# A seventh z tile inside the sample attention, the eighth behind it, in a one-core hybrid decoder step

## The chip, the cores and the metric

The kernel runs on one core of a Trainium2 chip. The metric is the device time of one execution in microseconds (us), as the median of several runs.

## What is computed

One layer of a decoder: an RMS norm, one input projection of width 1024 to 5648, three groups (a gated linear recurrence, a dilated-window attention, a state-space block) each with a gate, and one output projection. A prompt of 2048 tokens starts from empty state; eight samples of four tokens continue from a cache of 1024 positions. The parts that matter here:

```python
u = h @ w_in
x_lru, g_lru, q, k, v, g_attn, z, xbc, dt_raw = jnp.split(u, offs, axis=-1)
...
parts = [band_attn_sample(qh, k_all, v_all, W, slopes, wd, dl) for (wd, dl) in DILATIONS]
...
yg = (ys.reshape(Bn, L, D_SSD) * jax.nn.silu(z.astype(f32)))
```

`z` is 1024 columns wide and needs nothing but the normed input and the weights; it is used only at the end, in the state-space block. The kernel therefore uses its projection as filler work for TensorE in stages that would otherwise leave it idle.

## The kernel before

All matrices of the projections are split into a high and a low part, and every product is three matmuls (lines 82, 83 and 84). z is cut into eight tiles of 128 columns, here called z0 to z7. A tile loads its 512 KB of weights (`wr`, line 143), scales them on GpSimd (line 146), rounds the high part on ScalarE (`wh`, line 147) and takes the low part on VectorE (`wl`, line 148). Its matmuls fall into five pieces, one for each stretch of tokens, in the order 512, 512, 256, 288 and 512 tokens; a piece is 24 matmuls. ScalarE applies SiLU to a piece (`zo`, line 636) and the sync engine SP stores it (`d_z`, line 637). `z_tile` is a generator that yields after each piece.

The generator `zs` holds the pieces of the tiles meant for filling. The stage that advances the samples' state takes 14 of them (two of every three of its 20 steps). The samples' attention then runs: `fills()` walks eight parts (two heads by four samples each) through 80 steps. A part loads its cached keys (`kc` and `kf`) and values (`vt` and `vf`) and a bias (`sbias`), transposes the keys (line 911), computes scores in four column tiles (`sc`, line 932: 512 recent keys, then 128 far ones, then 32 new ones), does a softmax, transposes the weights `p` (line 954), multiplies by the values (`so`, line 966) and turns the result (`om`, line 973); a store of `ys` to `d_y` ends it. A loop over these steps decides at which of them the next z piece is taken.

Behind the attention, `z_end` holds the z tiles that are left, then frees their pools and loads the exp table. While it is walked, the scores of the first prompt unit (lines 1103 and 1124) are put between its pieces. The prompt attention has sixteen units; `load(i)` asks for the keys `k`, queries `q` and, with every fourth unit, a 1184 KB bias of unit i; `scores(i)` is one of seven steps, `exps(i)` the softmax. The bias's buffer lies in the memory of the samples' attention, so its load waits for that to be given up; `k` and `q` take buffers of the input tiles, which come free as the last z tiles finish with them.

Nothing runs in the order written: a scheduler at build time places the instructions of each engine by priority (mostly the order of the code) and by its own idea of when each can run. On the chip each engine, and SP's queue of transfers, then goes through its own list strictly in that order.

Of the kernel before, what the change touches and what calls it, by code (L numbers as in the profile page):

```python
# [22 lines left out]
CHUNKS = [(0, 512), (512, 512), (1024, 512), (1536, 256), (1792, 288)]  # L23
# [9 lines left out]
def tile_hybrid_step(ctx: ExitStack, tc: tile.TileContext, A):  # L33
# [121 lines left out]
    def project_steps(c0, evac, scale=1.0, order=CHUNKS):  # L155

        wh, wl = load_w(c0, scale)
        for t0, n in order:
            h_, l_, cols = xt(t0, n)
            ps = psA.tile([128, 512], F32, tag="mm", name="mm")  # L160
            for k in range(8):
                mm3(ps[:, :n], wh[:, k], wl[:, k], h_[k // 2][:, k % 2, cols], l_[k // 2][:, k % 2, cols], k == 0, k == 7)
            now = later[:]
            later.clear()
            for f in now:
                f()
            evac(ps, t0, n)
            for g in behind:
                next(g, None)
            yield  # L170
# [462 lines left out]
    def z_tile(pl, m):  # L633
        def evac(ps, t0, n):
            zt = pl.tile([128, 512], F32, tag="zo", name="zo", bufs=2)
            z_last.append(act.activation(out=zt[:, :n], in_=ps[:, :n], func=AF.Silu))
            sp.dma_start(out=d_z[128 * m:128 * m + 128, t0:t0 + n], in_=zt[:, :n])
        yield from project_steps(C_Z + 128 * m, evac, order=[CHUNKS[i] for i in (2, 1, 3, 4, 0)])
# [131 lines left out]

    zo_es = ExitStack()
    zo = zo_es.enter_context(tc.tile_pool(name="zo", bufs=1))
    zs = (None for m in range(6) for _ in z_tile(zo, m))


    with tc.tile_pool(name="cks", bufs=1) as ck:
# [92 lines left out]
    with tc.tile_pool(name="sa", bufs=1) as sa:  # L869
# [112 lines left out]
        def fills():  # L982

            parts = [sample_part(pr, bg) for pr in range(4) for bg in range(2)]
            for i, part in enumerate(parts):
                for j in range(6):
                    next(part)
                    yield
                    if i and j < 4:
                        next(parts[i - 1])  # L990
                        yield
            for _ in parts[-1]:
                yield

        for i, _ in enumerate(fills()):
            if i % 5 == 0:
                next(zs, None)
        for _ in zs:
            pass
# [28 lines left out]
            yield  # L1028

    def z_end():  # L1030
        zs = [z_tile(zo, m) for m in (6, 7)]
        for _ in CHUNKS:
            for z in zs:
                next(z, None)
                yield
        for z in zs:
            for _ in z:
                pass
        zo_es.close()
        wp_es.close()  # L1040
        with tc.issue_after(z_last[-1].ins):
            exp_ln = act.preload_act_table_set("natural_log_exp_and_others")
        ctx.enter_context(tc.issue_after(exp_ln.ins))
# [299 lines left out]
    def load(i):  # L1343
        if i < 16:
            next(units[i])

    def scores(i):
        return i >= 16 or next(units[i]) == "S"
# [4 lines left out]
    load(0)  # L1353
    load(1)
    s0 = False
    for i, _ in enumerate(z_end()):
        if i >= 6:
            for _ in range(3):
                s0 = s0 or scores(0)
    while not s0:  # L1360
        s0 = scores(0)
    ptp = es.enter_context(tc.tile_pool(name="ptp", bufs=8))
    load(2)
    while not exps(0):
        pass
    while not scores(1):
        pass
    next(units[0])
    for i in range(16):
        load(i + 3)  # L1370
# [279 lines left out]
```

## Time and profile before

| | us |
|---|---|
| median of 3 runs | 1965.07 (1964.24 to 1966.66) |
| the profiled execution, its own time | 1966.87 |
| its span, first to last instruction | 1965.1 |
| PE (TensorE matmul) busy | 1906.4, 97% of the span |
| DVE (VectorE) busy | 1065.2, 54% |
| ACT (ScalarE) busy | 780.9, 40% |
| samples' attention | about 981 to 1137 of the span |
| z6 and z7 with the first prompt scores | about 1137 to 1185 |

The profile is of one execution. PE's busy time is modelled, so a busy PE is not PE at its peak; a place where it is idle, or where its granted clock falls, is what the table above does not show and the rows below do.

### The profile page before, as it was taken

The numbers are of one execution on the slowest core, as the hardware profiler recorded it, in microseconds if no ns is written. First come the engines' busy times: TensorE is split into PE (matmuls) and PEld (weight loads), VectorE is DVE, ScalarE is ACT, GpSimd is POOL, SyncE is SP. The second block draws the span as 40 slices with busy tenths as digits, with TensorE's granted clock in tenths as the row PEclk, the third lists the DMA queues.
The fourth block names the chain that finished last, engine by engine and source line by source line (L and its number), as shares of the span: only waits on it lengthen the run. The fifth ranks groups of instructions, "written<-read, shape, count | busy, mean of one in ns | idle before, by whom it ended". The sixth has DMA issues, their size and how long they took to land.

```text
span 1965.1 us, 35826 instructions
## 1 busy us (share of the span) xinstructions
PE 1906.4 (97%) x14178; PEld 1559.9 (79%) x14178; DVE 1065.2 (54%) x2338; ACT 780.9 (40%) x1530; POOL 271.9 (14%) x346
## 2 busy tenths in 40 slices
PE   7999999999999999999999899999998999999998
PEld 7998888888888888887866686777776878677876
DVE  7414444444423666664322215666777777667774
ACT  6412637272712222223133315666564333324332
POOL 0100111111110111111000100000012232322231
PEclk9999999999999999998999999999999999999999
DMA  7422121121223222225477651442375444434441
GB/s 234 127 83 67 46 65 54 55 76 55 76 83 95 72 78 67 72 68 148 139 199 201 185 185 52 145 137 77 116 216 156 140 128 128 124 110 131 124 140 65
DMA packets 278388, 222.03 MB, mean 113 GB/s; under 512 B 34738, under 2 KB 234402, under 8 KB 278220
## 3 DMA queue, kind: packets, MB, share of 16 engines
q1 hardware_dynamic: 278220, 219.73, 37.3%
q8 instruction: 112, 1.84, 0.4%
q14 instruction: 56, 0.46, 0.1%
HBM read 150.81 MB, written 68.86 MB: 112 GB/s over the span
## 4 chain that ended last, share of the span: by engine, by line
PE 85%; DMA 4%; ACT 4%; DVE 3%; issue 1%; SPq 1%; POOL 1%; DVEq 0%; ACTq 0%; POOLq 0%
PE mm L82 15%; PE mm L84 15%; PE mm L83 15%; PE ops L84 5%; PE ops L83 5%; PE ops L82 5%; PE pt L1179 3%; ACT sr L1151 2%; PE o L1215 2%; PE s L1124 2%; PE yd L1298 2%; PE yo L1303 1%; PE s L1103 1%; DMA x<-in_x_prompt_dram 1%; PE mmt L82 1%
## 5 line engine op out<-in xcount | busy, mean ns | idle before, releaser
L82 PE MATMUL mm<-xh,wh 128*128 128x512 f32 (+2 forms) x1600 | 563.3, 352 | 1.6 <-DVE h L846 0.9
L83 PE MATMUL mm<-xl,wh 128*128 128x512 f32 (+2 forms) x1600 | 561.7, 351 | 0.0
L84 PE MATMUL mm<-xh,wl 128*128 128x512 f32 (+2 forms) x1600 | 561.0, 351 | 0.0
L82 PEld LDWEIGHTS mm<-xh,wh 128*128 128x128 f32 x1600 | 301.7, 189 | 44.0 <-issue 4.3
L84 PEld LDWEIGHTS mm<-xh,wl 128*128 128x128 f32 x1600 | 300.9, 188 | 41.0 <-issue 2.9
L83 PEld LDWEIGHTS mm<-xl,wh 128*128 128x128 f32 x1600 | 301.4, 188 | 39.0 <-issue 1.7
L146 POOL TENSOR_TENSOR wr<-wr,gC 128x1024 f32<-128x1024 f32 x40 | 79.1, 1978 | 415.7 <-DMA wr<-in_w_in_dram 370.8
L443 DVE SCALAR_TENSOR_TENSOR o<-u,ssdc,o 128x512 f32<-128x512 f32 (+1 forms) x216 | 128.8, 617 | 5.1
L1151 ACT ACTIVATE sr<-sr,nm 128x384 f32<-128x384 f32 (+3 forms) x128 | 97.9, 771 | 23.3 <-DVE nm L1147 14.1
L650 ACT ACTIVATE o<-o 128x512 f32<-128x512 f32 (+2 forms) x60 | 33.1, 552 | 149.4 <-DVE o L443 77.3
L148 DVE SCALAR_TENSOR_TENSOR wl<-wr,wh 128x1024 fp32r<-128x1024 f32 x40 | 48.9, 1223 | 68.4 <-ACT wh L147 68.4
L1062 ACT COPY ptsb<-pt 128x512 f32<-128x512 f32 x96 | 52.5, 583 | 75.0 <-PE pt L1179 74.9
L728 DVE TENSOR_SCALAR sg<-sg,cum 128x128 f32<-128x128 f32 (+1 forms) x256 | 72.9, 344 | 16.5 <-ACT ecB L726 16.5
L82 PE MATMUL mmt<-wh,xh 128*128 128x256 f32 (+3 forms) x272 | 78.5, 291 | 1.6 <-ACT xh L254 0.8
L83 PE MATMUL mmt<-wl,xh 128*128 128x256 f32 (+3 forms) x272 | 77.8, 287 | 0.3
L1179 PE MATMUL pt<-ident,sr 128*128 128x128 f32 x576 | 75.2, 281 | 2.8 <-ACT sr L1151 1.8
L84 PE MATMUL mmt<-wh,xl 128*128 128x256 f32 (+3 forms) x272 | 77.9, 288 | 0.0
L1112 DVE CUSTOM_DVE_ANT_1 sr<-s,bias 128x256 f32<-128x256 f32 x128 | 46.5, 419 | 56.9 <-PE s L1124 29.7
L441 DVE TENSOR_SCALAR o<-u,ssdc 128x512 f32<-128x512 f32 (+1 forms) x72 | 40.5, 575 | 65.8 <-ACT u L423 57.6
L1179 PEld LDWEIGHTS pt<-ident,sr 128*128 128x128 f32 x576 | 63.6, 143 | 15.1 <-issue 8.8
L423 ACT COPY u<-mm 128x512 f32<-128x512 f32 (+1 forms) x80 | 39.6, 495 | 88.6 <-PE mm L84 79.6
L726 ACT ACTIVATE ecB<-sg 64x512 f32<-64x512 f32 x60 | 37.8, 630 | 91.7 <-DMA sg<-d_cum 77.1
(526 smaller groups left out, 3585.0 us busy)
## 6 DMA issues: line engine op xcount, KB each, us to landing
wr<-in_w_in_dram SPq DMA_DIRECT2D x40, 512.0 KB
sg<-d_cum SPq DMA_DIRECT2D x30, 512.0 KB
d_xbc<-o SPq DMA_DIRECT2D x36, 256.0 KB
x<-in_x_prompt_dram SPq DMA_DIRECT2D x32, 256.0 KB
kc<-in_cache_attn_k_dram SPq DMA_DIRECT2D x32, 256.0 KB
vt<-in_cache_attn_v_dram SPq DMA_DIRECT2D x32, 256.0 KB
xres<-in_x_prompt_dram SPq DMA_DIRECT2D x32, 256.0 KB
out_dram<-ot SPq DMA_DIRECT2D x32, 256.0 KB
```

The lines of the kernel that those rows point to most:

```text
L82: pe.matmul(out, lhsT=wh, rhs=xh, start=start, stop=False)
L83: pe.matmul(out, lhsT=wh, rhs=xl, start=False, stop=False)
L84: pe.matmul(out, lhsT=wl, rhs=xh, start=False, stop=stop)
L146: pool.tensor_tensor(out=wr, in0=wr, in1=gC[:, :, None].to_broadcast([128, 8, 128]), op=OP.mult)
L148: dve.scalar_tensor_tensor(out=wl, in0=wr, scalar=scale, in1=wh.bitcast(F32), op0=OP.mult, op1=OP.subtract)
L441: dve.tensor_scalar(out=o, in0=v(0), scalar1=w[:, 0:1], scalar2=b, op0=OP.mult, op1=OP.add)
L443: dve.scalar_tensor_tensor(out=o, in0=v(t), scalar=w[:, t:t + 1], in1=o, op0=OP.mult, op1=OP.add)
L728: dve.tensor_scalar(out=sg[:n, h], in0=sg[:n, h], scalar1=cum[:n, c, 8 * g + h:8 * g + h + 1], scalar2=0.0, op0=OP.subtract, op1=OP.min)
L1062: act.copy(out=out, in_=in_)
L1112: dve.tensor_tensor_reduce(out=sr[e][r][:, nk:].rearrange("p (w c) -> p w c", w=2), in0=pw[e][:, j].rearrange("p (w c) -> p w c", w=2), in ...
L1151: act.activation(out=sr[e][r], in_=sr[e][r], func=AF.Exp, bias=nm[:, e, r:r + 1], accum_out=ll[:, e, r:r + 1])
L1179: pe.transpose(tp[:, r], sr[e][r][:, 128 * g:128 * g + 128], ident)
```

## The change

Seven tiles instead of six go into `zs`, the loop over the 80 attention steps takes 21 pieces instead of 16, evenly spread, and `z_end` has one tile in place of two that took turns. The scores of the first prompt unit may start after the second piece of z7 instead of the seventh of ten, and once they are through, those of the second unit may be taken between the pieces too.

```diff
-    zs = (None for m in range(6) for _ in z_tile(zo, m))
+    zs = (None for m in range(7) for _ in z_tile(zo, m))
...
         for i, _ in enumerate(fills()):
-            if i % 5 == 0:
+            if i * 21 % 80 < 21:
                 next(zs, None)
...
     def z_end():
-        zs = [z_tile(zo, m) for m in (6, 7)]
-        for _ in CHUNKS:
-            for z in zs:
-                next(z, None)
-                yield
-        for z in zs:
-            for _ in z:
-                pass
+        yield from z_tile(zo, 7)
...
     s0 = False
+    s1 = False
     for i, _ in enumerate(z_end()):
-        if i >= 6:
+        if i >= 1:
             for _ in range(3):
-                s0 = s0 or scores(0)
+                if not s0:
+                    s0 = scores(0)
+                elif i >= 4:
+                    s1 = s1 or scores(1)
...
-    while not scores(1):
-        pass
+    while not s1:
+        s1 = scores(1)
```

No instruction of the computation is added or removed. What moves is the order on the engines, and three places of it carry the prediction.

SP's list around the weights of z5, before. `wr` is that load; `d_z` is the store of z4's last piece; `kf`, `vt` and `vf` belong to the sixth part, `d_y` is the fifth part's result, and the rows behind `wr` are the seventh part's.

```order
L637 DMA d_z<-zo 128x512
L893 DMA kf<-in_cache_attn_k_dram 32x4x128 x4
L887 DMA vt<-in_cache_attn_v_dram 128x4x128 x4
L979 DMA d_y<-ys 128x16
L893 DMA vf<-in_cache_attn_v_dram 32x4x128 x4
L143 DMA wr<-in_w_in_dram 128x8x128
L899 DMA sbias<-in_c_sbias_dram 128x672
L887 DMA kc<-in_cache_attn_k_dram 128x4x128 x4
```

The same place of the changed kernel; the first `d_z` is z4's fourth piece, the second its last, and the other rows are the fifth part's.

```order
L899 DMA sbias<-in_c_sbias_dram 128x672
L887 DMA kc<-in_cache_attn_k_dram 128x4x128 x4
L637 DMA d_z<-zo 128x288
L143 DMA wr<-in_w_in_dram 128x8x128
L893 DMA kf<-in_cache_attn_k_dram 32x4x128 x4
L637 DMA d_z<-zo 128x512
L887 DMA vt<-in_cache_attn_v_dram 128x4x128 x4
```

The load stood behind the store of z4's last piece and thirteen further transfers; it now stands one piece ahead of that store.

PE's list where z4 ends, before: the last matmul of z4, then one whole part of the attention, then z5.

```order
L84 MATMUL mm<-xh_103,wl 128x512
L911 MATMUL tp<-ident,kc 128x128 x8
L954 MATMUL tp<-ident,p 128x128 x5
L954 MATMUL tp<-ident,p 32x128
L911 MATMUL tp<-ident,kc 128x128 x4
L966 MATMUL so<-vt,pt 32x128 x16
L966 MATMUL so<-vf,pt 32x128 x4
L966 MATMUL so<-vsn,pt 32x128 x4
L911 MATMUL tp<-ident,kc 128x128 x4
L973 MATMUL tp<-ident,om 128x128
L932 MATMUL sc<-ktT,qz 32x512
L911 MATMUL tp<-ident,kf 128x128 x4
```

The end of z4 in the changed kernel, and z5 from `xh_108` on.

```order
L84 MATMUL mm<-xh_103,wl 128x512
L911 MATMUL tp<-ident,kc 128x128 x4
L966 MATMUL so<-vt,pt 32x128 x16
L966 MATMUL so<-vf,pt 32x128 x4
L966 MATMUL so<-vsn,pt 32x128 x4
L911 MATMUL tp<-ident,kc 128x128 x4
L82 MATMUL mm<-xh_108,wh 128x512
L83 MATMUL mm<-xl_124,wh 128x512
L932 MATMUL sc<-ktT,qz 32x512
```

z5 follows z4 after half a part instead of a whole one with no filler in it.

PE's list at the large scores of an undisturbed part, before: one of the four column tiles, the transposes of `kf`, then the other three.

```order
L973 MATMUL tp<-ident,om 128x128
L932 MATMUL sc<-ktT,qz 32x512
L911 MATMUL tp<-ident,kf 128x128 x4
L932 MATMUL sc<-ktT,qz 32x512 x3
```

The third part of the changed kernel:

```order
L84 MATMUL mm<-xh_111,wl 128x512
L911 MATMUL tp<-ident,kf 128x128 x4
L932 MATMUL sc<-ktT,qz 32x512 x4
L932 MATMUL sc<-ktT,qz 32x128 x4
L932 MATMUL sc<-ksn,qz 32x32 x4
```

Counted over the eight parts, the 32 large score matmuls stand in 18 groups before (four in the first part, two in each other) and in 12 in the changed kernel (one group of four in parts two, three, six and eight).

From the first prompt scores on, PE's list is the same but for the z pieces between the first unit's scores (256 and 288 columns where 288 and 512 stood); the second unit's scores stand behind the last z piece in both kernels.

## Rows read from the trace of the kernel before

**Rows 1.** The page's busy time, share of the span and instructions of each engine.

```profile
PE 1906.4 (97%) x14178; PEld 1559.9 (79%) x14178; DVE 1065.2 (54%) x2338; ACT 780.9 (40%) x1530; POOL 271.9 (14%) x346
```

**Rows 2.** Windows: stretch, its length, busy time by engine, PE clock, DMA share, GB/s.

```profile
1070.00:1080.00 10.00, 6.13 (x70) 4.27 (x70) 2.14 (x4) 3.47 (x6) 0.00 (x0) 0.83 0.81 232
1080.00:1090.00 10.00, 3.32 (x32) 1.36 (x30) 3.00 (x12) 2.82 (x4) 2.38 (x4) 0.92 0.81 229
```

**Rows 3.** PE's timeline, 1067 to 1096: start, length, instruction, idle before and releaser.

```profile
1067.65 0.24 PE L932 MATMUL sc<-ksn,qz 128*32 128x32 f32 x8
...
1069.78 0.40 PE L84 MATMUL mm<-xh,wl 128*128 128x512 f32 x1
1072.35 0.63 PE L911 MATMUL tp<-ident,kc 128*128 128x128 f32 x4 [2.17 <-DMA kc<-in_cache_attn_k_dram]
1074.46 0.82 PE L911 MATMUL tp<-ident,kc 128*128 128x128 f32 x4 [1.48 <-DMA kc<-in_cache_attn_k_dram]
...
1090.03 0.45 PE L911 MATMUL tp<-ident,kc 128*128 128x128 f32 x1 [6.71 <-DMA kc<-in_cache_attn_k_dram]
1091.25 0.80 PE L82 MATMUL mm<-xh,wh 128*128 128x512 f32 x1 [0.77 <-ACT wh L147]
...
1093.53 0.63 PE L83 MATMUL mm<-xl,wh 128*128 128x512 f32 x1
1093.95 0.63 PE L84 MATMUL mm<-xh,wl 128*128 128x512 f32 x1
...
1095.47 0.40 PE L82 MATMUL mm<-xh,wh 128*128 128x512 f32 x1
1095.70 0.40 PE L83 MATMUL mm<-xl,wh 128*128 128x512 f32 x1
```

**Rows 4.** SP's queue, 1066 to 1098: start of an issue, length, transfer.

```profile
1072.16 0.34 SPq L637 DMA_DIRECT2D d_z<-zo  x1
...
1083.72 0.39 SPq L143 DMA_DIRECT2D wr<-in_w_in_dram  x1
```

**Rows 5.** Timelines of POOL and ACT, 1082 to 1092.

```profile
1088.21 1.90 POOL L146 TENSOR_TENSOR wr<-wr,gC 128x1024 f32<-128x1024 f32 x1 [4.05 <-DMA wr<-in_w_in_dram]
...
1090.14 1.06 ACT L147 ACTIVATE wh<-wr 128x1024 fp32r<-128x1024 f32 x1 [4.73 <-POOL wr L146]
```

**Rows 6.** PE's timeline in an undisturbed part, 1026 to 1032.

```profile
1026.70 1.08 PE L966 MATMUL so<-vt,pt 128*32 128x128 f32 x32
...
1028.28 0.66 PE L911 MATMUL tp<-ident,kc 128*128 128x128 f32 x4
...
1029.09 1.05 PE L932 MATMUL sc<-ktT,qz 128*32 128x512 f32 x2
1030.06 0.65 PE L911 MATMUL tp<-ident,kf 128*128 128x128 f32 x4
1030.65 1.06 PE L932 MATMUL sc<-ktT,qz 128*32 128x512 f32 x6
1031.64 0.50 PE L83 MATMUL mm<-xl,wh 128*128 128x512 f32 x1
1031.97 0.39 PE L84 MATMUL mm<-xh,wl 128*128 128x512 f32 x1
```

**Rows 7.** PE's timeline, end of the attention and first prompt scores.

```profile
1136.48 0.27 PE L973 MATMUL tp<-ident,om 128*128 128x128 f32 x1
...
1165.54 1.27 PE L1103 MATMUL s<-k,q 64*32 64x128 f32 x40
```

**Rows 8.** SP's queue, 1136 to 1144.

```profile
1137.22 0.35 SPq L979 DMA_DIRECT2D d_y<-ys  x1
1138.83 0.38 SPq L1070 DMA_DIRECT2D bias<-in_c_bias_dram  x1
```

**Rows 9.** Windows over the same end, columns as in rows 2.

```profile
1137.00:1185.00 48.00, 48.00 (x390) 40.25 (x397) 5.48 (x35) 4.72 (x10) 0.00 (x0) 1.00 0.60 189
1140.00:1148.00 8.00, 8.00 (x37) 6.63 (x36) 0.00 (x0) 1.20 (x2) 0.00 (x0) 1.00 0.94 337
```

## Prediction

> **What bounds the kernel now.** The page's first table comes first: PE is busy 97% of the span [rows 1], so no other engine can be the bound over the whole, and moving matmuls cannot pay by itself; only a hole in PE's list can be filled, or PE's own work made shorter. The next view is the windows of 10 us over the stage that the change touches. Nearly all show PE busy for 10 of 10 us; two do not, 6.13 and 3.32 us, and the granted clock is below 1 in them [rows 2]. PE's timeline there tells what is missing. z4's last matmul starts at 1069.78. Then comes a whole part of the attention with no z in it, and z5 starts at 1091.25. On the way PE waits 2.17, 1.48 and 6.71 us for cached keys and 0.77 us for z5's weights [rows 3], 11.1 us in all.
>
> Why z5 is so late is read on the queues. SP issues z5's weights at 1083.72 [rows 4], 14 us after z4 had ended, since that load stands behind the whole sixth part's loads and a store of the fifth part's result. From the issue it takes 4.5 us to GpSimd's start, 1.9 us there and 1.1 us on ScalarE [rows 5]: 7.5 us to PE. The long wait for keys is of the same kind: they are issued behind these 512 KB.
>
> The hole also costs clock. Behind it matmuls of 512 columns start 0.42 us apart, which is the lower of the two levels, 1.2 GHz; from 1095.47 on it is 0.23 us, at 2.4 GHz [rows 3]. Nine z matmuls and a transpose start in the 4.2 us from 1091.25 to 1095.47; at the faster spacing they take 2.1 us, so 2.1 us are lost. The windows 1070 to 1090 also show a clock of 0.83 and 0.92 [rows 2]; on some 9 us of work I put 1 us to that, an estimate.
>
> **The hole: 14.2 us to gain.** In the new order SP issues z5's weights before z4's last piece is stored, and PE has filler in every part. If nothing takes the hole's place, 11.1 + 2.1 + 1 = 14.2 us go.
>
> Does the load come in time? It stands behind the store of z4's fourth piece, which ScalarE can write only after the part's exp and a table load. Before, the store in that position went out 1072.16 - 1067.83 = 4.3 us after the part's last score matmul [rows 3, 4] (1067.65 and 0.18 to the next start). So the load goes at 4.8 us, PE can have the weights at 4.8 + 7.5 = 12.3 us. What stands on PE in that time in the new order: 19 matmuls of 288 columns and 9 of 512, then fifteen more of 512, four sets of key transposes, one of `p` and one `so`. At 0.227 us for 512 columns, and 0.128 for 288 by their ratio, that is 2.4 + 5.4 us; a set of transposes is at most 0.6 (kf: 1030.06 to 1030.65), `p` about 0.8 by its six transposes, `so` 1.6 (1026.70 to 1028.28) [rows 6]. The sum is 2.4 + 5.4 + 2.2 + 0.8 + 1.6 = 12.4 us. It is even, to 0.1 us, so some wait is likely: 1.4 MB of `sbias` and `kc` are queued ahead (128 x 672 floats, and four times 128 x 512), and at the 229 GB/s of that window [rows 2] they run about 6 us. I take 1 us, between 0 and the 6.7 us of the worst wait seen [rows 3].
>
> **The score groups: 5.8 us to gain.** One large score matmul alone holds PE from 1029.09 to 1030.06, 0.97 us; three in a row, on three column tiles, from 1030.65 to 1031.64, 0.99 us [rows 6]. A group costs the same however many tiles it has, so 18 groups becoming 12 save 6 x 0.97 = 5.8 us of PE's own time. A group of four at this size is not in the trace; the bounds are 0.99 us, and 1.31 if the fourth adds a third of the three. In the second part the group follows its last key transposes at once and must wait for that copy: I take 0.6 us off for it. Lower bound of this term: 5.8 - 4 x 0.32 - 0.6 = 3.9.
>
> The Trainium skill, TensorEngine Tiling, "Key Properties", says that a change of tiling mode drains the engine, which speaks against strewing z pieces between column-tiled matmuls. The trace agrees that a return costs something: behind a score group the first two z starts are 0.33 us apart instead of 0.23 [rows 6]. Counted in the order, the changes of mode fall from 68 to 52 while the borders between z and other work rise from 86 to 98. By the rule the change would gain 16 x 0.1 = 1.6 us more, and by the borders it loses 12 x 0.1 = 1.2 us; I leave both out of the sum.
>
> **The other part of the attention: -1.6 us.** Keys of a part are issued behind its `sbias`, which waits for the former part's softmax to have read the old one. Before, the first keys came 1072.35 - 1067.83 = 4.5 us after the last score matmul, the second set at 6.6 us [rows 3]. In the new order the fifth part wants them after 2.4 + 2.0 = 4.4 us and after about 5.5: a wait of 1.1 us. The fourth part's are wanted at 3.4 (loaded ahead) and about 5.9. I add 0.5 us for one place more, in the second part, where a quarter of `kf` stands behind a z store. Bounds: 0, and 5 us if each of three parts waits as the first two waits above did.
>
> **The end of the stage: nothing.** z6's matmuls used to cover the loads of the prompt attention; this cover is gone. Before, 29 us of z lay between the turn of the last part's result at 1136.48 and the first prompt score at 1165.54 [rows 7]; now 45 matmuls, 10.2 us, do. The bias is needed by VectorE some 1.4 us later, at 11.6. The store of `ys` goes 0.7 us after 1136.48 and the bias at 2.35 us [rows 8]; `k`, `q` and `k` now go ahead of it. Together they are 768 KB (three times 128 x 512 floats) and 1184 KB, 5.8 us at the 337 GB/s seen while they ran [rows 9]. With the first bytes at about 2.5 us they are in at 8.3, 3 us early. At the 189 GB/s of the whole stretch [rows 9] they are in at 12.8, 1.2 us late; that is the other bound. The scores of the first unit then lie between pieces of 256 and 288 columns instead of 288 and 512; the first stretch between them is the same length (10 matmuls at about 0.12 for 9 at 0.13). Those of the second unit have not moved on PE, so that third edit is worth nothing, either way.
>
> **Sum.** -14.2 - (5.8 - 0.6) + 1 + 1.6 = -16.8 us. The profiled execution's own time is 1966.87 and gives 1950.1; the median is 1.8 below it, so 1948.3 us, -0.85%.
>
> **Rivals.** First, the hole only moves: z5's weights come late by as much as in the worst wait, 6.7 us, and the clock falls as it did, 2.1 us, while the score groups still gain. 1948.3 - 1 + 8.8 = 1956. For it speaks the even balance above and the 1.4 MB ahead; against it that the other two loads, z6's and z7's, now stand a whole piece or more ahead.
>
> Second, the end is crowded. Some 9.1 MB ran in 1137 to 1185 (189 GB/s for 48 us [rows 9]). In the new order about 27 us of PE work lie from the last part to the end of z7 and 12 more until the third prompt unit's scores. If the transfers kept to 189 GB/s they would need 48 us for 39: PE waits up to 9 us, 1957. Against it: most of these bytes (values, the second bias) are needed later, and 337 GB/s has been seen.
>
> Third, on the other side: the same crowding at a lower rate. SP's list is strict, so a prompt unit's keys wait behind everything. The gain of 16.8 us is used up, and the kernel slower by the 3.9 us that count, once the 9.1 MB need 39 + 20.7 = 60 us, that is below 152 GB/s. The stretch now runs at 0.60 of DMA's time [rows 9], which speaks against it; 1970.
>
> Fourth, the change does not do what it says: the hole stays whole because the scheduler's order meets another late load, and only the groups gain: 1965.1 - 5.2 = 1960, up to 1965 if they are worth nothing.
>
> **Chances.** The forecast, 1944.5 to 1952: 0.62. The hole moved or the end crowded, 1952 to 1961: 0.26. Nothing much, within 0.2% (3.9 us, about what a measurement of this kernel can tell from no change): 0.06. Slower: 0.06. So faster is 0.88. The low end is the sum with no new wait and the groups whole, 1965.1 - 20 = 1945, and 1 us under it for the estimated clock term. The high end takes in most of the second case: 1957.
>
> **What would show it.** In the new profile PE's windows of the attention should show no stretch below 9 of 10 us and a clock of 1; `kc` as a releaser of PE should fall from 10.4 us to 1 or 2, and the wait for `wh` to about 1. Score groups of four should take about 1 us. The time from the last `om` to the first prompt score should be near 10 us. I am wrong if PE stands still before z5, z6 or z7 for over 4 us, if `bias` or `k` appears as a releaser of the prompt scores, or if a group of four takes twice one of three.

## The result, and the profile after

| | before | changed |
|---|---|---|
| median (lowest to highest) | 1965.87 us (1964.24 to 1969.55, 4 runs) | 1946.14 us (1941.76 to 1949.98, 4 runs) |
| profiled execution: span, own time | 1965.1, 1966.87 us | 1948.2, 1949.98 us |
| PE busy in the profile | 1906.4 us | 1898.8 us |

The ratio is 0.9898, with a 95% interval of 0.9877 to 0.9919: 19.7 us by the medians, 16.9 by the two spans; 16.8 was forecast. That the two spans agree with the forecast so closely is chance: of the stretch that the change touches they show 20.1 us less (below), and 3.2 of these are hidden by a later start of the attention (987.95 against 986.49) and a longer rest of the program (768.8 against 767.1). The page's row of busy times, which answers to [rows 1]:

```profile
PE 1898.8 (97%) x14178; PEld 1561.5 (80%) x14178; DVE 1065.3 (55%) x2338; ACT 779.6 (40%) x1530; POOL 269.6 (14%) x346
```

The windows where the hole was, columns as in [rows 2], and one window earlier:

```profile
1060.00:1070.00 10.00, 8.54 (x72) 5.09 (x71) 2.02 (x3) 2.13 (x3) 1.90 (x1) 0.83 0.76 194
1070.00:1080.00 10.00, 10.00 (x64) 7.34 (x63) 2.90 (x11) 3.31 (x5) 0.59 (x3) 1.00 0.48 138
1080.00:1090.00 10.00, 10.00 (x110) 8.73 (x109) 2.02 (x6) 3.62 (x7) 0.00 (x0) 1.00 0.84 236
```

PE's waits from 970 to 1210: engine, tile and line, what it waited for, us in total, times, longest. The cached keys, 10.4 us in three waits before, are gone from the list; `wh` is what is left of the hole. The window at 8.54 goes against one sign of the prediction (no stretch below 9 of 10, and a clock of 1).

```profile
PE s L1096 <- DVE mx L1121: 2.1, 2, 1.5
PE pt L1172 <- ACT sr L1144: 1.6, 2, 1.3
PE mm L82 <- ACT wh L147: 1.5, 1, 1.5
PE mm L82 <- DVE h L846: 0.9, 1, 0.9
PE s L1117 <- DVE mx L1105: 0.7, 1, 0.7
```

Where that wait comes from is read in the timelines of SP, POOL and PE, which answer to [rows 4, 5]. z5's weights are issued 27 us earlier than before. GpSimd starts 6.2 us after the issue, not 4.5, and PE comes to a stand. Behind the wait one score group and three z matmuls run at the lower clock: the group of one takes 1.84 us to the next start, against 0.97 [rows 6].

```profile
1056.37 0.38 SPq L143 DMA_DIRECT2D wr<-in_w_in_dram  x1
...
1062.54 1.90 POOL L146 TENSOR_TENSOR wr<-wr,gC 128x1024 f32<-128x1024 f32 x1 [10.30 <-DMA wr<-in_w_in_dram]
...
1065.57 0.50 PE L82 MATMUL mm<-xh,wh 128*128 128x512 f32 x1 [1.46 <-ACT wh L147]
1065.91 0.40 PE L83 MATMUL mm<-xl,wh 128*128 128x512 f32 x1
1066.24 1.92 PE L932 MATMUL sc<-ktT,qz 128*32 128x512 f32 x2
1068.08 0.80 PE L84 MATMUL mm<-xh,wl 128*128 128x512 f32 x1
1068.68 0.63 PE L82 MATMUL mm<-xh,wh 128*128 128x512 f32 x1
1069.11 0.63 PE L83 MATMUL mm<-xl,wh 128*128 128x512 f32 x1
1069.53 0.44 PE L84 MATMUL mm<-xh,wl 128*128 128x512 f32 x1
```

The end of the attention on PE, SP and VectorE, which answers to [rows 7, 8]: 10.4 us from the last `om` to the first prompt score, and VectorE reads that score the moment that PE has it. The bias, issued 2.65 us behind `om` with `k`, `q` and `k` ahead of it, is no releaser.

```profile
1139.45 0.27 PE L973 MATMUL tp<-ident,om 128*128 128x128 f32 x1
...
1149.86 0.46 PE L1096 MATMUL s<-k,q 64*32 64x128 f32 x9
...
1142.10 0.38 SPq L1063 DMA_DIRECT2D bias<-in_c_bias_dram  x1
...
1151.16 0.42 DVE L1105 CUSTOM_DVE_ANT_1 sr<-s,bias 128x256 f32<-128x256 f32 x1 [11.00 <-PE s L1096]
```

**An account of PE's list.** The stretch from the first key transposes of the attention to the end of the last z matmul holds the same work in most kernels here. I gave each row of PE's timeline the time to the next row's start, less the wait that this next row records, and added these up by kind. This takes the waits apart from the work, and it leaves out how far the rest of the program varied: from the first matmul of `pt` with the values (L1208) to the end of the span, the profiles of these kernels show 762 to 772 us.

| us | whole stretch | recorded waits | score groups (`sc`) | transposes | z | `so` | prompt scores |
|---|---|---|---|---|---|---|---|
| before | 198.3 | 11.3 | 20.8 | 28.8 | 120.3 | 12.8 | 4.1 |
| changed | 178.2 | 1.5 | 16.2 | 24.5 | 119.0 | 13.0 | 3.9 |

So the stretch became 20.1 us shorter: 9.8 of waits, 4.6 of score groups, 5.6 of transposes and z.

### The profile page after: what moved, and what is told of

Read it like the earlier page. It is cut to its first block, busy times and chain, and to the rows that moved or that the text cites. A ratio compares the mean times of both kernels' runs of the same rounds, so it can differ in the third digit from the quotient of the medians.

```text
span 1948.2 us, 35823 instructions
## 1 busy us (share of the span) xinstructions
PE 1898.8 (97%) x14178; PEld 1561.5 (80%) x14178; DVE 1065.3 (55%) x2338; ACT 779.6 (40%) x1530; POOL 269.6 (14%) x346
## 3 DMA queue, kind: packets, MB, share of 16 engines
q8 instruction: 112, 1.84, 0.4%
## 4 chain that ended last, share of the span: by engine, by line
PE 83%; ACT 5%; DMA 4%; DVE 4%; issue 2%; SPq 1%; POOL 1%; DVEq 0%; ACTq 0%; POOLq 0%
PE mm L82 15%; PE mm L84 15%; PE mm L83 15%; PE ops L84 5%; PE ops L83 5%; PE ops L82 5%; PE pt L1172 3%; PE o L1208 2%; ACT sr L1144 2%; PE s L1117 2%; PE yd L1291 2%; PE yo L1296 1%; PE s L1096 1%; PE mmt L82 1%; DMA x<-in_x_prompt_dram 1%
## 5 line engine op out<-in xcount | busy, mean ns | idle before, releaser
L1121 DVE CUSTOM_DVE_ANT_0 sr<-s,bias 128x128 f32<-128x128 f32 (+3 forms) x128 | 58.7, 486 | 23.4 <-PE s L1117 22.7
```

Source lines behind the costliest of these rows:

```text
L1121: dve.tensor_tensor_reduce(out=sr[e][r][:, :nk], in0=ps[e][:, :nk], in1=bs[:, e, 512 - nk:512], scale=1.0, scalar=NEG, op0=OP.add, op1=OP. ...
```

## The experiments

Each ratio is to the kernel before, timed beside it on the same chip; its medians there were 1967.1 to 1969.1.

**1. The hole alone.** z5's weights asked for behind z4's fourth piece, in the kernel before (`w` is handed to the next `z_tile`):

```
+    for j, _ in enumerate(z_tile(zo, m, w)):
+        if j == 3:
+            w = load_w(C_Z + 128 * (m + 1)) if m == 4 else None
...
```

> The kernel before with one thing moved: z5's weights are asked for behind z4's fourth piece, ahead of the sixth part's loads, instead of behind them. Six tiles still lie in the attention, two behind it, and the scores of the first prompt unit where they were. One score group joins another (18 groups to 17). The theory of the prediction (the hole is one late load): the 14.2 us of hole and clock go, minus a wait of 0 to 2, and one group of 0.97 us: 1950 to 1954 us beside 1965.9 of before, PE's windows from 1070 to 1090 above 9 of 10, and kc gone as a releaser of PE. The rival (the gain of the change comes from spreading the pieces evenly and from the seventh tile, and the hole would only move to the eighth part): 1960 to 1966.

Measured: 1965.3 us, ratio 0.9993 (0.9982 to 1.0004): nothing that this measurement can tell. The timelines of SP and PE show why the test was not yet clean, and more:

```profile
1067.54 0.39 SPq L143 DMA_DIRECT2D wr<-in_w_in_dram  x1
...
1074.45 2.01 PE L919 MATMUL tp<-ident,kc 128*128 128x128 f32 x8 [4.49 <-DMA kc<-in_cache_attn_k_dram]
1076.11 0.78 PE L82 MATMUL mm<-xh,wh 128*128 128x512 f32 x1
```

The load stood behind a part's values in SP's list and went 2 us before z4's end. But PE waited for keys even so, and then twice more at the end of the attention (1.7 us for `wh` and 0.9 for `wl`), where z5 had now been used up. Recorded waits in the account: 8.8 us of the 11.3 are still there.

**2. The load much earlier.** The same with `j == 0`.

> The kernel before with z5's weights asked for behind z4's first piece, three pieces earlier than in the first run of this kind, where SP still issued them only at 1067.54, 2 us before z4's end. Here they lie in SP's list in the fourth part, so they cannot be late. Six tiles in the attention, as before; in PE's list the z pieces now run out in the seventh part, and the eighth has none. If the hole is a late load (the prediction's reading): it is gone, 1950 to 1954. If the hole is a want of filler (a part's 2.6 MB of keys, values and bias take 11 to 12 us at 229 GB/s, its own PE work about 5, and six tiles do not hold enough z for eight parts): it moves whole to the eighth part, PE waits there for kc 5 to 12 us with a lower clock, and the time is 1960 to 1966.

Measured: 1965.97 us, ratio 0.9976 (0.9963 to 0.9988), 4.7 us less. One score group joined another here, but since it then waits for the copy of its keys the account has only 0.2 us for it (20.8 to 20.6). SP issues the weights at 1038.16, in the fourth part, and no window between 1010 and 1100 shows PE below 9.99. The hole is at the end of the attention now. The windows there, columns as in [rows 2]:

```profile
1100.00:1110.00 10.00, 8.75 (x58) 5.78 (x56) 2.91 (x10) 5.18 (x7) 0.59 (x3) 1.00 0.85 239
1110.00:1120.00 10.00, 6.76 (x91) 3.98 (x92) 3.84 (x13) 3.92 (x8) 0.00 (x0) 1.00 0.72 178
1120.00:1130.00 10.00, 7.42 (x61) 4.80 (x60) 2.59 (x5) 1.47 (x3) 1.89 (x1) 0.56 0.30 79
```

PE's timeline in the same stretch:

```profile
1108.80 0.63 PE L919 MATMUL tp<-ident,kc 128*128 128x128 f32 x4 [1.00 <-DMA kc<-in_cache_attn_k_dram]
...
1119.56 0.85 PE L962 MATMUL tp<-ident,p 128*128 128x128 f32 x6 [3.04 <-DVE p L955]
1120.97 1.73 PE L974 MATMUL so<-vt,pt 128*32 128x128 f32 x32 [0.57 <-DVE pt L885]
...
1126.15 0.79 PE L82 MATMUL mm<-xh,wh 128*128 128x512 f32 x1 [1.57 <-ACT wh L147]
```

Keys are only 1.0 us of it. PE waits 3.0 us for the part's own softmax (VectorE, the exponential, VectorE again) and then for each copy behind it, with the clock at 0.56. So a part without z makes a hole wherever it lies, and the late load was not all of the hole. It was some of it: the account's waits fall from 11.3 to 6.9 us. How much of the 10.4 us for keys was the load's this run does not tell, since behind the eighth part there are no keys to wait for.

**3. The two halves of the change.** The spacing left as it was, with all else changed; and the spacing alone, in the kernel before:

```
 changed:  -            if i * 21 % 80 < 21:
           +            if i % 5 == 0:
 before:   -            if i % 5 == 0:
           +            if i * 21 % 80 < 21:
```

> The changed kernel without its spacing: seven tiles' pieces in the attention and the scores of two units between the pieces of the eighth, but a piece at every fifth step, as before, and what is left behind the last step. PE's list in the eight parts is then that of the kernel before, piece for piece, and z5's weights lie where they lay in SP's list. If the gain is filler in every part: nothing of it is left, 1963 to 1968 beside 1966 to 1969 of before, and PE stands still 10 to 12 us before z5. If the seventh tile in the attention or the new end is what pays: 1950 or less.

Measured: 1968.51 us, ratio 1.0000 (0.9988 to 1.0012). PE's waits from 970 to 1180 and the window of the hole are nearly those of before. With a piece at every fifth step the seventh tile never gets among the eight parts: sixteen pieces are taken there, as before, and the others stand behind the last step. So the run shows that neither the new end nor a tile less in `z_end` has the gain; it says nothing on more z at the old spacing. The first of the waits:

```profile
PE tp L911 <- DMA kc<-in_cache_attn_k_dram: 9.7, 3, 6.6
```

The window:

```profile
1080.00:1090.00 10.00, 3.44 (x30) 1.37 (x29) 2.94 (x11) 3.19 (x5) 2.49 (x4) 0.91 0.85 239
```

> The kernel before with the new spacing alone: 21 pieces over 80 steps, but only six tiles, so that the pieces run out in the seventh part and the eighth has none; z6 and z7 behind the attention as before. 18 large score groups become 13 here, 4.9 us, and z5's weights are asked for in the fifth part. If a part without filler makes a hole wherever it lies: PE stands still 5 to 8 us in the seventh and eighth part, with a lower clock there, and about the group term and some of the hole are gained: 1955 to 1961. If spacing with an early load is enough: the whole gain, 1945 to 1949.

Measured: 1957.15 us, ratio 0.9949 (0.9934 to 0.9964), 10 us less: half of it. The waits are those of run 2, in the part without z, with the clock at 0.50 in the window 1120 to 1130:

```profile
PE tp L954 <- DVE p L947: 3.0, 1, 3.0
PE pt L1179 <- ACT sr L1151: 1.6, 2, 1.3
PE mm L82 <- ACT wh L147: 1.4, 2, 1.1
PE tp L954 <- ACT ktT L875: 1.1, 1, 1.1
```

So neither edit has the gain by itself. In the account the spacing alone leaves 6.8 us of waits, the tile alone 10.7, both 1.5. In waits, then, the spacing alone is worth nearly what the early load of run 2 was (6.9 left); its further gain is 4.2 us in score groups (16.4 against 20.6) and 1.6 in transposes. The seventh tile adds the z that is missing at the end.

How z lies over the eight parts is seen by its time on PE from one part's turn (`om`) to the next, counted as in the account; the first stretch begins with the first key transposes:

| us of z in stretch | 1 | 2 | 3 | 4 | 5 | 6 | 7 | 8 |
|---|---|---|---|---|---|---|---|---|
| before | 14.3 | 10.0 | 10.0 | 10.1 | 3.2 | 13.3 | 7.0 | 8.3 |
| load much earlier (run 2) | 14.3 | 9.9 | 10.0 | 12.0 | 9.8 | 10.3 | 5.6 | 0 |
| spacing alone | 14.4 | 10.0 | 13.4 | 15.2 | 9.0 | 9.8 | 5.2 | 0 |
| changed | 14.3 | 10.0 | 13.4 | 15.9 | 9.0 | 14.7 | 10.9 | 8.1 |

The waits lie where this is 5.6 or less: 3.9 us in stretch 5 of before and 7.5 in stretch 6, ahead of its z; 1.3 and 4.0 us in stretches 7 and 8 of run 2, 1.4 and 4.0 of the spacing alone. In the stretches with 7.0 us or more nothing else waits, but for z's own weights (1.5 us in stretch 4 of the changed kernel, 0.3 of the spacing alone). Six tiles hold 72 to 77 us here, 9 and more for each stretch. So it is not shown that six are too few: six tiles spread evenly, with z5's load in time, were not tried.

**4. Fewer bytes.** As run 2, but each part loads keys and values of two of its four samples and uses them for all four.

```
+                if i == 0:
...
                     load_rows(kt_, A["cache_attn_k"], pr, bg, 2 * i)
...
-            for i in range(2):
-                load_rows(vt[i], A["cache_attn_v"], pr, bg, 2 * i)
+            load_rows(vt[0], A["cache_attn_v"], pr, bg, 0)
```

> As the run with the load much earlier, but each part loads the keys and values of two of its four samples only and uses them for all four (the other two samples' 1 MB of keys and values is left out): 1.6 MB a part instead of 2.6. Six tiles, PE's own work unchanged. If want of filler under the transfers is the hole's cause: at 229 GB/s a part needs 7 us instead of 11.5, the filler of six tiles is enough, kc goes as a releaser, and the time falls to 1950 to 1954 without a seventh tile. If the transfers do not bind and the hole is made by order and waits alone: it stays as in that run, 1960 to 1966.

Measured: 1951.89 us, ratio 0.9908 (0.9891 to 0.9926), 14.1 us below run 2 by the medians. PE's waits from 970 to 1180 in full:

```profile
PE pt L1188 <- ACT sr L1160: 1.6, 2, 1.3
PE mm L82 <- DVE h L854: 0.9, 1, 0.9
```

Six tiles are filler enough for shorter parts. (With its bias a part's transfers are 2.97 MB, not the 2.6 of the expectations: 13 us at 229 GB/s, and 8.4 us for the 1.92 MB of this run.) With the loads the order of PE's list changed too: z lies evenly over the eight parts here (7.0 to 11.8 us in each stretch), where run 2 uses it up in seven. The run therefore shows that a part's transfers, together with the order made for them, make the hole, but not how much of that is the transfers' time on the chip and how much the order that was made for them.

**5. Score groups alone.** In the kernel before, a part's score matmuls stand behind its last key transpose: eight groups of four instead of 18.

```
+                        kt = pe.transpose(tp[:, j], kt_[:, h, j], ident)
...
+            with tc.issue_after(kt.ins):
               for o0, n, k0 in ((0, 512, 0), (1, 128, 512), (1, 32, None)):
```

> The kernel before with one thing moved: the large score matmuls of a part stand behind its last key transposes, so each part has one group of four; 18 groups become 8. z and its weights' loads stay, and so does the hole. The theory (a group costs 0.97 us however many column tiles it has): 10 x 0.97 = 9.7 us less, minus waits for the last keys' copy of up to 0.6 in each of eight parts: 1956 to 1961. The rival (a fourth matmul adds a third of three, so that a group of four costs 1.31): 9.7 - 8 x 0.33 = 7.1, minus the same waits, 1959 to 1964. If single matmuls hide behind others' work in some way: no change, 1966.

Measured: 1960.76 us, ratio 0.9969 (0.9957 to 0.9981), 6.1 us less (3.7 to 8.5). On PE the groups save 10.5 us in the account (20.8 to 10.3), so a group of four costs no more than one of three. But the stretch is only 8.0 us shorter: the recorded waits rise from 11.3 to 13.0, and the windows from 1060 to 1090 stand at a clock of 0.77, 0.72 and 0.62: PE is through with a part's work earlier and waits longer where filler is missing.

**6. The third edit, and the early scores.** The changed kernel without scores(1) between z7's pieces; and with the first unit's scores held back as well, until z7 is through:

```
 -                elif i >= 4:
 -                    s1 = s1 or scores(1)
```
```
 -        if i >= 1:
 +        if i >= 9:
```

> The changed kernel without its third edit: no scores of the second prompt unit between z7's pieces, all of them behind z7; all else as changed. The theory: nothing, within 0.2% of the changed kernel's 1946.1, since the trace of the changed kernel shows the second unit's first score matmul at 1166.09, behind the last z matmul at 1165.77, as it is here. The rival (the edit moves VectorE's or the queues' work although not PE's): 2 to 4 us slower, 1948 to 1950.

> The changed kernel with the scores of the first prompt unit held back until z7 is through; nothing else is moved. What their place between the pieces is worth: in the changed kernel VectorE's readings of these scores take 5.7 us (1151.16 to 1154.0 and 1156.31 to 1159.1) and PE's scores about 4, and PE never waits for VectorE in that stretch. Held back, PE has only three score buffers and must go at VectorE's rate: 1.7 us, and the second unit's scores start that much later. The exponentials do not start earlier or later, since they stand behind the last z piece's table load (1166.86, 1.28 us) in either. The theory of a small price: 1 to 3 us slower than 1946.1, 1947 to 1949. The rival (the early start is a main part of the gain, by about the 8 us between the first and the last of these scores): 1954.

Measured: 1947.17 us, 0.9893 (0.9876 to 0.9910), and 1946.97 us, 0.9896 (0.9876 to 0.9915). The changed kernel, run again below, gave 0.9906 (0.9889 to 0.9924). Neither has a price that shows; the 1 to 3 us that I gave the second were too many.

**7. An eighth tile.** The changed kernel with all of z in the attention, 26 pieces over the 80 steps.

```
-    zs = (None for m in range(7) for _ in z_tile(zo, m))
+    zs = (None for m in range(8) for _ in z_tile(zo, m))
...
-            if i * 21 % 80 < 21:
+            if i * 26 % 80 < 26:
...
-        yield from z_tile(zo, 7)
+        yield from ()
```

> The changed kernel with the eighth tile of z in the attention too, 26 pieces over its 80 steps and none behind it; the scores of the first two prompt units follow the last part's result directly. If filler pays only where PE stands still under transfers: there are 1.5 us of waits left to fill in the attention, and a score group fewer or two (9 large groups instead of 12) gives 2 to 3; against it the first prompt scores' loads lose the 10.2 us of z over them. From the last result's turn these loads take 8.3 us at 337 GB/s and 12.8 at 189, so PE stands still for 8 to 13 us and its clock falls for some more: 1950 to 1958 beside 1946 of the changed kernel. If every tile moved into the attention pays as the seventh did: 1930 to 1940. If the loads at the end go at 152 GB/s or less (the prediction's third rival): 1960 or more.

> The changed kernel as it is, on the same chip as the run with eight tiles, to compare that one and the variants with: 1946 within 3, a ratio of 0.988 to 0.991.

Measured: 1949.16 us, 0.9912 (0.9897 to 0.9928), beside 1948.56 us, 0.9906 (0.9889 to 0.9924), of the changed kernel: no difference, just under the expected range. The groups gave back more than the 2 to 3 us that I took: 4.7 in the account (16.2 to 11.5). PE, SP and VectorE at the end:

```profile
1151.36 0.33 PE L973 MATMUL tp<-ident,om 128*128 128x128 f32 x1 [0.41 <-DVE om L970]
...
1160.93 1.14 PE L1117 MATMUL s<-k,q 64*32 64x128 f32 x24 [7.61 <-DVE mx L1105]
...
1153.82 0.38 SPq L1063 DMA_DIRECT2D bias<-in_c_bias_dram  x1
...
1159.66 0.42 DVE L1105 CUSTOM_DVE_ANT_1 sr<-s,bias 128x256 f32<-128x256 f32 x1 [7.53 <-DMA vn<-d_v]
```

VectorE can read the first score 8.3 us after the last `om`, and PE stands still 7.6 us for it. The bias is issued 2.5 us after that `om`, 1.7 us behind the store of `ys`, and the reading waits for a transfer: the records name `vn`, but line 1105 reads only the scores, which PE had finished, and the bias, so the bias is what had to come. What is missing here is the cover that the changed kernel still has in z7.

**8. One group in every part, from the changed kernel,** with the edit of run 5; and with z5's weights earlier as well (the edit of run 1, with `j == 1`).

> The changed kernel with the large score matmuls of every part behind its last key transposes: one group of four in each part, 12 groups become 8; nothing else is moved. By the prediction's term 4 x 0.97 = 3.9 us less; by the run of the groups alone, where 10 groups less took 7.8 us off PE's busy time (1906.4 to 1898.6), 3.1 us less. If the stage is bound by PE now, this comes through whole: 1942 to 1943 beside 1946 to 1947 of the changed kernel and of its two variants. If it comes back as waits, as part of it did in the groups alone (there the span fell by 7.7 and PE's waits for keys rose from 10.4 to 11.6), 1945 to 1947.

> The changed kernel with one group of four in every part and with z5's weights asked for behind z4's second piece, a third of a tile earlier or more; nothing else is moved. The changed kernel still waits 1.2 to 1.5 us for these weights, and in one profile the window 1060 to 1070 shows a clock of 0.83. If the early load takes this away: 1.5 to 3 us below the run with the groups alone, 1939 to 1941.5, and no wait for wh in the attention. If it only moves 512 KB ahead of keys and makes PE wait for these instead: the same as with the groups alone, 1943, with kc as a releaser of PE again for 1 to 2 us.

Measured: 1938.09 us, 0.9846 (0.9824 to 0.9867), and 1942.28 us, 0.9859 (0.9840 to 0.9878). The first is the fastest kernel of the study, and its interval lies wholly below those of the changed kernel. In the account its stretch is 8.7 us shorter than the changed kernel's: 6.0 in the score groups (16.2 to 10.2, with the one at the lower clock and the copy's wait in the second part gone too), 1.1 in waits, 1.6 elsewhere. Its order also has SP ask for z5's weights 5 us earlier, counted from the attention's first key transposes (63.2 us behind them instead of 68.4), and ahead of a z store; the wait for `wh` is gone:

```profile
1046.60 0.67 SPq L143 DMA_DIRECT2D wr<-in_w_in_dram  x1
...
1052.75 1.90 POOL L146 TENSOR_TENSOR wr<-wr,gC 128x1024 f32<-128x1024 f32 x1 [8.62 <-DMA wr<-in_w_in_dram]
```

Asked for earlier still, at 1031.23, these 512 KB lie among the fourth part's keys. PE's waits name `tp` behind ScalarE's copy of keys for 1.9 us then, two windows stand at 9.21 and 8.92, and the kernel is no faster than with the groups alone.

## Why the prediction came out as it did

**The size: near, from terms that were off in both directions.** By the account:

| us | predicted | measured |
|---|---|---|
| waits: the hole's 11.1 less new ones (1 + 1.6) | -8.5 | -9.8 |
| slow clock in and behind the hole | -3.1 | -5.6 in transposes and z, with what PE loses at changes between kinds of work |
| score groups | -5.2 | -4.6 |
| sum | -16.8 | -20.1 |

The waits: 1.5 us are left instead of 2.6. The weights' own wait was sized at 1 us and was 1.46; their load went out 5.05 us behind the part's last scores (4.8 predicted), and it was the 6.2 us to GpSimd that were long, with the transfers that I had named ahead of it. The fifth part's keys, for which I took 1.1, did not wait at all.

The clock: the estimate of 1 us on 9 us of work was too small. How much of the 5.6 us belongs to the borders between kinds of work instead can be estimated. Changes between column-tiled matmuls (`sc` and `so`, 128*32 in the rows) and others fall from 68 to 52, and to 34 in the first kernel of run 8. The Trainium skill, TensorEngine Tiling (Array Packing), "Key Properties", has PE drain at a change of tiling mode. From 52 to 34, transposes, z, `so` and prompt scores fall by 1.6 us together, of which 0.7 to 0.8, by the slow z rows shown above, is the clock behind the wait for `wh`. So the trace agrees with a cost, but a small one: 0.04 to 0.09 us a change, at most the 0.1 that I had read from the rows. Sixteen changes are then 0.7 to 1.4 us, and the hole's clock and slow rows 4.2 to 4.9 instead of 3.1. Read from the rows themselves the clock's share is smaller: in the hole the six transposes of `p` take 1.6 us (0.6 to 0.9 elsewhere) and a set of key transposes 1.05 (0.53), and the nine z matmuls behind it 1.7 us more than at 0.227 each, some 3 us together, near the 3.1 predicted. No run measured either share by itself, so the split stays open.

The groups: 12 in place of 18, and 4.6 us instead of 5.2, since the one at the lower clock gave back 0.87. A group of four with its 128-column matmuls takes 1.10 us; the second part's, which must wait for its keys' copy, takes 1.61, as the 0.6 us off for it had it:

```profile
1010.88 1.68 PE L932 MATMUL sc<-ktT,qz 128*32 128x512 f32 x8
1012.49 0.40 PE L84 MATMUL mm<-xh,wl 128*128 128x288 f32 x1
...
1032.83 1.28 PE L932 MATMUL sc<-ktT,qz 128*32 128x512 f32 x16
1033.93 0.24 PE L932 MATMUL sc<-ksn,qz 128*32 128x32 f32 x8
```

**The cause: half wrong.** The step that failed is "why z5 is so late is read on the queues". I took the late load for the hole's cause, and filler in every part for something that followed. Run 2 put the load in time (run 1 only in part), and the hole moved to the end and left 6.9 us of waits of 11.3: the load was a part of it. The hole is a part without z. In the kernel before, PE's list has used up one tile before it may begin the next; with the load in time, the six tiles are used up before the eighth part, in the order that the scheduler makes of them. My sum held because the change removes the hole on both grounds, and the sum did not have to tell them apart, which is luck; the forecast for run 1, from the first ground alone, was 11 us off and more.

**The end: as predicted.** 10.4 us of cover (10.2 predicted) and no wait. Run 7 has the bias at 8.3 us, the same figure as in the prediction, but by chance: `k` and `q` were issued some 27 us ahead of the last `om` there, and the values ran beside the bias, at 258 GB/s in all. (The prediction's 5.8 us for 1952 KB are 5.9 with 1024 bytes to the KB; and its high end, 1952, does not reach the 1957 of its second rival, most of which it is said to take in.) The third edit is worth nothing, as said. Of the rivals the first (the hole only moves) is what run 2 shows for the load alone; in the changed kernel its price is the 1.46 us and the slow rows behind them, not 8.8. The second and third, a crowded end, were not seen in the changed kernel; run 7 shows where that end begins. Nor was the fourth: no second late load kept the hole whole.

## What to carry to other kernels

A stall at a late load shows what came last, not all that is missing. Ask first what PE would have had to do there if the load had been in time, and count the filler of each stage against what the stage's own chain needs, on the same rows. It is the filler in each part that counts: handed out too fast it runs out before the end, and then the hole is only elsewhere. Work taken off an engine that waits in the same stage comes back in part as waiting (run 5: 10.5 us off the groups, 8.0 off the stretch), and comes through once the waits are gone (run 8: 6.0 off the groups, 8.7 off the stretch).

## What had not been expected of the hardware

The prediction had only three column tiles to go by; four, too, run in nearly the time of one: a group of four large score matmuls with its four small ones takes 1.10 us, a single large one 0.97. Not expected at all: a single wait of 1.46 us was followed by rows at the lower clock (0.83 in the window), and so it was when the changed kernel was run again (1.58 us, 0.83), while the same wait of 1.17 and 1.23 us in the two kernels of run 6 was followed by none (1.00 in every window of the attention).
